# Two heads of a neighbourhood pair in one two-bank score tile, and transposes three units behind the scores

## The chip, the cores and the metric

The kernel runs on one core of one Trainium2 chip. The metric is device time in microseconds (us) of one execution. One execution computes one layer of a bidirectional encoder.

PE is the matrix engine, PEld its weight loads, DVE the vector engine, ACT the scalar engine, POOL the general engine, SP the engine whose queue issues nearly all transfers. PSUM is the memory of eight banks into which PE writes its results; DVE and ACT read them there.

## The reference, cut to what matters

The layer has two attentions over 1024 prompt tokens and 256 sample tokens, eight heads each: a neighbourhood attention (kind "n" below) and a latent attention (kind "m"). Each is scores, a softmax, and the weighted sum of values.

```python
# neighbourhood: each token looks at a window of rows and columns, with a bias
sc = jnp.einsum('bwhd,bxwyhd->bhwxy', q_r, k_nb, preferred_element_type=jnp.float32) * scale
sc = sc + bias.transpose(0, 2, 1, 3)[None].astype(jnp.float32)
p = jax.nn.softmax(sc.reshape(b, h, GRID_W, kh * NA_KW), axis=-1)
return jnp.einsum('bhwxy,bxwyhd->bwhd', p, v_nb)
...
# latent: each token looks at all tokens, in blocks of 128 queries
p = jax.nn.softmax(sc * scale, axis=-1).astype(v.dtype)
return jnp.einsum('bhqk,bkhd->bqhd', p, v)
...
# behind both: projection of each branch, a sigmoid gate from the input, merge,
# output projection, then a mixture of experts
```

## The kernel before

The program runs in stages: projections (up to 481 us of the span), attention (481 to 907), merge of the branches, routing, experts (about 1200 to 1815) and a last norm. Only the attention loop changes.

**Units.** One unit is one head (h = 2p + x, x = 0 or 1) and one block of 128 queries (qi). The two heads of a pair follow each other, so an even unit has x = 0 and an odd one x = 1. Units 0 to 63 are the latent prompt, 64 to 127 the neighbourhood prompt, 128 to 159 the sample. An "m" prompt unit has 1024 keys, in two blocks of 512, each in its own PSUM bank; an "n" prompt unit has 384 keys (256 for the first and the last block), so it fills less than one bank.

**The loop.** Iteration i does, in the order in which each engine's queue receives them: `scores` of unit i (PE) and its `maximum` (DVE; for "n" one instruction that adds the bias, writes the sum to an SBUF slot and takes the maximum, then a short read of the accumulator), `transpose` of unit i-LOOK (PE into PSUM, then a copy by ACT), `exp` of unit i (ACT), `normalize` of unit i (a reciprocal on DVE, then a multiplication on POOL), and, when unit i-LOOK-1 has x = 1, `pv` of that pair (PE). With LOOK = 2, `pv` falls into the even iterations. Then `load_at` may issue the transfers that load the next job (a head pair's q, k, v and bias), and `fill` gives PE some of 384 matmuls of the gate projection, spread over 146 iterations, so two or three an iteration (mean 2.63).

**The fill.** `piece_gates` works in pieces of 24 matmuls, so a piece lasts about nine iterations. In the middle of a piece (n == 12) the weights of the next are split into a rounded half and a remainder: a cast by ACT (L654) and a subtraction by DVE (L655), both 128x1024. These are called a burst here; in the neighbourhood prompt they come in iterations 68, 77, 86, 95, 104, 114 and 123. At a piece's end ACT copies the result out of PSUM (L682) and SP stores it to `gate_d` (L683).

**Score tiles.** `psS` has two buffers of two banks each. Every unit takes one, whatever it fills. So the scores of unit i wait until DVE has read those of unit i-2. The other four banks are taken by the transposes (2), the `pv` result (1) and the fill (1).

**Slots.** All larger SBUF data lies in 49 slots of 128x1024 that are handed out in the order in which they came free: `sl.get` and `sl.put`. A slot given back right behind the issue of a store from it is waited for by its next writer until that store has landed. The queue of SP is in order: a store to `gate_d` that stands behind a job's loads is issued behind them.

Of the kernel before, what the change touches and what calls it, by code (L numbers as in the profile page):

```python
# [10 lines left out]
F32 = mybir.dt.float32  # L11
# [84 lines left out]
def kernel(ctx, tc, A, out_p, out_s, upto=99, dbg=None):  # L96
# [14 lines left out]
    def pool(name, bufs=1, space=None, stack=None):  # L111
        kw = dict(name=name, bufs=bufs, reuse_waits="tile")
        if space is not None:
            kw["space"] = space
        return (stack or ctx).enter_context(tc.tile_pool(**kw))
# [698 lines left out]
    class Job:  # L814
# [45 lines left out]
        def vat(b, kt, h, w):  # L860
            o = kt * b.nh * 64 + (h - b.h0) * 64
            return b.v[:w, o:o + 64]

    class Unit:


# [15 lines left out]

        def scores(u):

            u.s = psS.tile([128, 2, 512], F32, name="s")
            q, k = u.job.q[u.h], u.job.k[u.h]
            qs = slice(u.qi * 128, u.qi * 128 + 128)
            for b in range(u.nb):
                ks = slice(u.t0 * 128 + b * u.w, u.t0 * 128 + (b + 1) * u.w)
                if u.kind == "m":  # L890
                    ops = [(q[0][:96, qs], k[0][:96, ks]), (q[0][:96, qs], k[1][:96, ks]), (q[1][:96, qs], k[0][:96, ks])]
                else:
                    ops = [(q[0][:, qs], k[x][:, ks]) for x in range(2)]
                for n, (a, c) in enumerate(ops):
                    PE.matmul(u.s[:, b, :u.w], a, c, start=(n == 0), stop=(n == len(ops) - 1))  # L895
# [37 lines left out]
    def pv(a, b):  # L933

        half = a.qi % 2
        key = (a.kind, a.p, a.job.g)
        if half == 0:
            oacc[key] = fps["o"][:, oturn[0] % 2, :]
            oturn[0] += 1
        o = oacc[key]  # L940
        cs = slice(half * 128, half * 128 + 128)
        for i in range(0, a.n, 128):
            w = min(128, a.n - i)
            for u in (a, b):
                PE.matmul(o[64 * u.x:64 * u.x + 64, cs], u.job.vat(u.t0 + i // 128, u.h, w), v3(u.P, 8)[:w, i // 128, :],  # L945
                          start=(i == 0), stop=(i + 128 >= a.n), tile_position=(0, 64 * u.x), skip_group_check=True)
        sl.put(a.P, b.P)
        if half:
            os = sl.get(F32R)
            t = os[:, :512].rearrange("p (x n) -> p x n", x=2)  # L950
            S.copy(t[:, 0], o)
            V.tensor_sub(t[:, 1], o, f32(t[:, 0]))
            tk = (SP if a.job.g else 0) + (a.qi - 1) * 128
            SY.dma_start(ao_d[a.kind][:, a.p * 128:a.p * 128 + 128, tk:tk + 256].rearrange("x r n -> r x n"), f32(t))
            sl.put(os)
        if b.last:
            sl.put(*b.job.t)
# [106 lines left out]
    psS = pool("psS", bufs=2, space=PSUM, stack=astack)  # L1064
# [2 lines left out]
    fps["o"] = psO.tile([128, 2, 256], F32, name="o")  # L1067
    fps["p"] = pool("psF", bufs=1, space=PSUM, stack=astack)

    LOOK = 2  # L1070
    LO, LS = (5, 5, 5, 5, 4, 4, 4), (4, 6, 4, 7)
    load_at = {16 * j + LO[j]: [jobs[j + 1]] for j in range(7)}
    load_at.update({16 * 7 + LS[0]: [jobs[8]], 16 * 7 + LS[1]: [jobs[9]], 128 + LS[2]: [jobs[10]], 128 + LS[3]: [jobs[11]]})
# [2 lines left out]
    merge = Merge()  # L1076
    for i in range(n + LOOK + 2):
        u = units[i] if i < n else None
        w = units[i - LOOK] if 0 <= i - LOOK < n else None
        z = units[i - LOOK - 1] if 0 <= i - LOOK - 1 < n else None  # L1080
        if u:
# [8 lines left out]
        if z and z.x:  # L1090
            pv(units[i - LOOK - 2], z)
        for j in load_at.get(i, []):
# [667 lines left out]
```

## Time and profile before

| | |
|---|---|
| time before, median of 3 runs | 1855.91 us (1853.6 to 1859.47) |
| the profiled execution | 1854.83 us |
| its span in the trace | 1853.1 us |
| mean granted clock of PE, as a share of full speed | 0.973 |
| PE busy | 94% of the span |
| attention in the span | 481 to 907 us |
| neighbourhood prompt units | about 723 to 853 us |

The span begins with the first instruction and ends with the last; the time of the execution is 1.7 us longer. In the rows further down a first number is the start in us from the span's start, the second the duration. A bracket tells how long the engine had been idle and which instruction ended that. "xN" is the number of instructions in a row that were put together.

### The profile page before, as it was taken

How to read it: one execution, taken by the hardware profiler on the slowest of the kernel's cores; microseconds unless marked ns; L12 is line 12 of the kernel's file. 1: busy time of each engine (PE TensorE's matmuls, PEld its weight loads, DVE VectorE, ACT ScalarE, POOL GpSimd, SP SyncE). 2: the span in 40 equal slices, each digit the busy share in tenths (PEclk: the TensorE clock that was granted, in tenths of full speed). 3: DMA queues.
4: the chain of work that ended last, by engine and by line, in shares of the span. 5: the costliest groups of instructions: out<-in, count | busy, mean ns of one | idle time of the engine just before them, and what ended most of it. 6: DMA issues, size and time to landing. Idle time of an engine off the chain costs nothing.

```text
span 1853.1 us, 27078 instructions
## 1 busy us (share of the span) xinstructions
PE 1743.1 (94%) x9874; PEld 1357.6 (73%) x9874; DVE 1001.4 (54%) x1674; ACT 838.8 (45%) x1391; POOL 319.0 (17%) x329
## 2 busy tenths in 40 slices
PE   5999999999999999999899999699999999999991
PEld 4787777998888888767688877567676676766760
DVE  6324422111455655444357466777777777777764
ACT  6222222321455555666533213366556565655642
POOL 0010210000122222322333000111111111111110
PEclk9989999999999999999899999799999999999995
DMA  9335676536714442878977356899999999999916
GB/s 349 109 115 168 222 264 221 191 91 165 152 55 112 115 121 86 232 214 230 297 251 224 132 216 235 327 359 360 361 365 360 362 356 361 358 356 364 349 36 242
DMA packets 268848, 439.47 MB, mean 237 GB/s; under 512 B 31928, under 2 KB 131592, under 8 KB 268712
## 3 DMA queue, kind: packets, MB, share of 16 engines
q1 hardware_dynamic: 252008, 389.45, 62.8%
q0 software_dynamic: 13824, 37.77, 7.3%
q10 hardware_dynamic: 2880, 10.49, 1.4%
q8 instruction: 79, 1.29, 0.3%
q14 instruction: 57, 0.47, 0.1%
HBM read 367.53 MB, written 82.67 MB: 243 GB/s over the span
## 4 chain that ended last, share of the span: by engine, by line
PE 84%; DVE 5%; DMA 5%; issue 2%; ACT 2%; SPq 1%; POOL 1%; DVEq 0%; POOLq 0%; ACTq 0%; another core or an unknown queue 0%
PE ph L1540 19%; PE pg L432 13%; PE py L1566 11%; PE s L895 6%; PE pw L1303 5%; PE fp L766 5%; PE fp L678 4%; PE o L945 4%; PE tp L927 4%; PE pg L599 3%; PE pt L1527 2%; PE pg L341 1%; PE pg L557 1%; PE pt L1553 1%; DMA x_d<-s,idx 1%
## 5 line engine op out<-in xcount | busy, mean ns | idle before, releaser
L1540 PE MATMUL ph<-s,s 128*128 128x512 f32 x1536 | 377.0, 401 | 1.4 <-DVE s L1530 1.2
L1399 ACT CAST s<-s 128x1024 fp32r<-128x1024 f32 x256 | 265.9, 1055 | 194.2 <-PE ph L1540 193.9
L1540 PEld LDWEIGHTS ph<-s,s 128*128 128x128 f32 x1536 | 286.4, 188 | 73.8 <-issue 13.9
L1400 DVE TENSOR_TENSOR s<-s,s 128x1024 fp32r<-128x1024 f32 x256 | 304.5, 1221 | 63.7 <-ACT s L1399 57.4
L432 PE MATMUL pg<-s,s 128*128 128x512 f32 (+1 forms) x1416 | 270.2, 351 | 7.8 <-ACT s L182 4.2
L432 PEld LDWEIGHTS pg<-s,s 128*128 128x128 f32 x1416 | 226.8, 190 | 53.0 <-ACT s L182 4.9
L1566 PE MATMUL py<-s,aT 128*128 128x512 f32 x512 | 225.1, 592 | 0.7 <-ACT aT L1555 0.7
L917 POOL TENSOR_SCALAR s<-s,m 128x1024 f32<-128x1024 f32 (+2 forms) x160 | 122.8, 767 | 438.5 <-DVE m L916 363.6
L1566 PEld LDWEIGHTS py<-s,aT 128*128 128x128 f32 x512 | 94.8, 190 | 108.2 <-issue 100.0
L895 PE MATMUL s<-s,s 96*128 96x512 f32 (+2 forms) x592 | 147.7, 368 | 1.8 <-ACT s L913 1.4
L913 ACT ACTIVATE s<-s,m 128x1024 f32<-128x1024 f32 (+2 forms) x160 | 124.9, 781 | 46.6 <-DVE m L903 27.3
L929 ACT COPY s<-tp 128x512 f32<-128x512 f32 (+2 forms) x160 | 78.2, 488 | 120.5 <-PE tp L927 116.9
L895 PEld LDWEIGHTS s<-s,s 96*128 96x128 f32 (+1 forms) x592 | 109.9, 190 | 27.9 <-ACT s L913 2.3
L678 PE MATMUL fp<-s,s 128*128 128x512 f32 x384 | 126.4, 430 | 2.8 <-ACT s L682 2.6
L927 PE MATMUL tp<-ident,s 128*128 128x128 f32 x752 | 110.4, 275 | 9.8 <-POOL s L917 9.4
L183 DVE TENSOR_TENSOR s<-s,s 128x1024 fp32r<-128x1024 f32 x31 | 37.7, 1224 | 148.7 <-ACT s L182 137.0
L1303 PE MATMUL pw<-s,s 128*128 128x512 f32 x480 | 118.0, 400 | 0.0
L766 PE MATMUL fp<-s,s 128*128 128x512 f32 (+1 forms) x576 | 114.0, 359 | 2.8 <-DMA s<-ao_m 1.4
L903 DVE TENSOR_REDUCE m<-s 128x1 f32<-128x1024 f32 (+1 forms) x80 | 85.0, 1062 | 51.6 <-PE s L895 50.2
L1572 POOL DMA_INDIRECT x_d<-s,idx x32 | 71.7, 2242 | 231.1 <-DVE s L1571 116.1
L766 PEld LDWEIGHTS fp<-s,s 128*128 128x128 f32 x576 | 96.5, 191 | 20.1 <-DMA s<-ao_m 2.1
L927 PEld LDWEIGHTS tp<-ident,s 128*128 128x128 f32 x752 | 89.3, 141 | 25.3 <-POOL s L917 15.9
(225 smaller groups left out, 2012.3 us busy)
## 6 DMA issues: line engine op xcount, KB each, us to landing
s<-in_expert_w SPq DMA_DIRECT2D x384, 512.0 KB
s<-in_w_in SPq DMA_DIRECT2D x47, 512.0 KB
s<-in_ada_w POOLq DMA_DIRECT2D x32, 512.0 KB, 6.1
s<-nak_d SPq DMA_DIRECT2D x40, 256.0 KB
s<-in_x_prompt SPq DMA_DIRECT2D x16, 512.0 KB
s<-in_ada_w SPq DMA_DIRECT2D x16, 512.0 KB
s<-gate_d SPq DMA_DIRECT2D x16, 512.0 KB
gate_d<-s SPq DMA_DIRECT2D x16, 384.0 KB
```

What stands on the lines that cost most here:

```text
L432: PE.matmul(p[:m, :CHUNKS[c][1]], g.at(a, j, 0, m), b.at(j, c), start=(j == 0 and n == 0), stop=(j == KD - 1 and n == 2))
L678: PE.matmul(p, w.at(a, j), b.at(j, 0), start=(n == 0), stop=(n == 23))
L766: PE.matmul(p[:, :w], b.ws[i].at(u, x * 4 + j), o[:, v, :w], start=(m == 0), stop=(m == 11))
L895: PE.matmul(u.s[:, b, :u.w], a, c, start=(n == 0), stop=(n == len(ops) - 1))
L913: S.activation(u.out, u.src, AF.Exp, bias=u.m[:, 0:1], scale=u.sign, accum_out=u.m[:, 1:2])
L917: G.tensor_scalar(u.P[:, :u.n], u.P[:, :u.n], u.m[:, 2:3], 1.0, op0=OP.mult, op1=OP.mult)
L927: PE.transpose(tp[:w, i // 128, :], u.P[:, b * 512 + i:b * 512 + i + w], ident)
L1303: PE.matmul(b.p, x[b.c].at(k, b.c, b.k), w[:, k % 2, :], start=(k + i == 0), stop=(k == 7 and i == 2))
L1399: S.copy(hi, r)
L1400: V.tensor_sub(lo, r, f32(hi))
L1540: PE.matmul(p, a[:, 2 * q + k, :], v3(w, 2)[:, k, :], start=(q + k + i == 0), stop=(q == 3 and k == 1 and i == 2))
L1566: PE.matmul(p, b.aT_[:, k, :], w[:, hb * 512:hb * 512 + 512], start=(k == 0), stop=(k == 3))
```

## The change

The two heads of a neighbourhood pair get one score tile between them: the head with x = 0 writes the first bank, the one with x = 1 the second. The latent units keep a tile each. And LOOK becomes 3, in both attentions: the transposes of a unit stand three iterations behind its scores, `pv` four, which puts `pv` into the odd iterations.

```diff
+    pairs = [None]
+
     class Unit:
...
         def scores(u):
 
-            u.s = psS.tile([128, 2, 512], F32, name="s")
+            if u.kind == "m" or u.x == 0:
+                pairs[0] = psS.tile([128, 2, 512], F32, name="s")
+            u.s = pairs[0] if u.kind == "m" else pairs[0][:, u.x:u.x + 1]
             q, k = u.job.q[u.h], u.job.k[u.h]
...
-    LOOK = 2
+    LOOK = 3
```

In the changed kernel the lines behind `scores` stand four further down (L895 becomes L899, L907 L911, L927 L931, L945 L949, L954 L958); L654, L655, L678, L682 and L683 keep their numbers. In the rows below a name with a number is one buffer or tile, the text in brackets what the instruction waits for, by the engine or transfer queue that has to finish.

The first place is PE's queue, units 92 and 93, the end of a `pv` and the second head's scores, before:

```order
L945 MATMUL o_3905<-s48_6960,s7_6518 64x128
L945 MATMUL o_3905<-s23_6983,s7_6518 64x128
L678 MATMUL fp_7061<-s47_399,s37_6936 128x512 [waits Activation_49]
L678 MATMUL fp_7061<-s31_413,s37_6936 128x512
L678 MATMUL fp_7061<-s47_399,s15_6937 128x512
L678 MATMUL fp_7061<-s47_399,s37_6936 128x512
L895 MATMUL s_7068<-s33_6512,s8_6509 128x384 [waits DVE_49]
L895 MATMUL s_7068<-s16_6515,s8_6509 128x384
L927 MATMUL tp_7074<-ident_63,s41_7026 128x128 [waits PE_49,Pool_49]
L927 MATMUL tp_7074<-ident_63,s41_7026 128x128 x2
```

The same two units in the changed kernel, from the first head's scores to those of the second and the start of the `pv` behind them:

```order
L899 MATMUL s_7022<-s28_6492,s3_6489 128x384
L899 MATMUL s_7022<-s15_6495,s3_6489 128x384
L931 MATMUL tp_7028<-ident_63,s37_6959 128x128 [waits PE_49,Pool_49]
L931 MATMUL tp_7028<-ident_63,s37_6959 128x128 x2
L678 MATMUL fp_7036<-s47_399,s42_6910 128x512 [waits Activation_49]
L678 MATMUL fp_7036<-s31_413,s42_6910 128x512
L678 MATMUL fp_7036<-s47_399,s1_6911 128x512
L678 MATMUL fp_7036<-s47_399,s42_6910 128x512
L899 MATMUL s_7022<-s8_6501,s13_6498 128x384 [waits DVE_49]
L899 MATMUL s_7022<-s25_6504,s13_6498 128x384
L931 MATMUL tp_7048<-ident_63,s44_6981 128x128 [waits PE_49,Pool_49]
L931 MATMUL tp_7048<-ident_63,s44_6981 128x128 x2
```

Both heads write the tile s_7022. The first waits for no engine; the second waits for DVE, whose last instruction on that tile is the first head's maximum (L911) just ahead. Before, the wait of the second head (tile s_7068) was for the unit two earlier. And `pv` stands behind the second head's scores now, where it stood behind the first one's.

The second place is DVE's queue at units 108 and 109, before (slot and score tile are the first names behind the operation and the arrow):

```order
L907 ISA s13_7409,m_7410<-s_7406,s20_6886 128x384 [waits PE_49,Pool_49]
L907 ISA m_7410 128x1
L916 RECIPROCAL m_7410<-m_7410 128x1 [waits Activation_49]
L907 ISA s26_7431,m_7432<-s_7428,s42_6888 128x384 [waits PE_49,Pool_49]
L907 ISA m_7432 128x1
```

And in the changed kernel, from the end of unit 107 to unit 108:

```order
L920 RECIPROCAL m_7356<-m_7356 128x1 [waits Activation_49]
L956 TENSOR_TENSOR s11_7372<-o_3905,s11_7372 128x256 [waits Activation_49]
L911 ISA s46_7382,m_7383<-s_7379,s4_6867 128x384 [waits DMAHW7_49,PE_49,Pool_49]
L911 ISA m_7383 128x1
L920 RECIPROCAL m_7383<-m_7383 128x1 [waits Activation_49]
```

The maximum of unit 108 now writes slot s46 and waits for a transfer from it. That transfer stands in SP's queue, in the changed kernel, behind the loads of the next job:

```order
L807 DMA s16_7215<-nak_d 64x1024 [waits DMAHW3_49]
L844 DMA s18_7218<-vna_d 128x8x128 [waits DMAHW4_49]
L857 DMA s48_7220<-in_nbias 128x768 [waits DMAHW5_49]
L857 DMA s33_7222<-in_nbias 128x768 [waits DMAHW6_49,PE_49,Pool_49]
L683 DMA gate_d<-s46_7225 128x512 [waits DMAHW7_49,Activation_49]
L650 DMA s6_7250<-in_w_in 128x8x128 [waits DMAHW0_49,PE_49,Pool_49]
```

Before, the store at this place was from slot s24, and the next to write s24 was the copy L682 of the piece that ends in iteration 109, on ACT, with the same wait. In the same way the maximum of unit 124 waits in the changed kernel for the store of the piece that ends in iteration 118, and the subtraction L655 of iteration 95 for an `ao_n` store.

## Rows read from the trace of the kernel before

**Rows 1.** The page: busy us of each engine, share of the span, instructions.

```profile
PE 1743.1 (94%) x9874; PEld 1357.6 (73%) x9874; DVE 1001.4 (54%) x1674; ACT 838.8 (45%) x1391; POOL 319.0 (17%) x329
```

**Rows 2.** Busy time by stretch: columns in the first line; stretches of attention.

```profile
core 0: us, PE busy (x) PEld busy (x) DVE busy (x) ACT busy (x) POOL busy (x), PEclk, DMA share, GB/s
...
500.00:723.00 223.00, 223.00 (x1871) 189.66 (x1870) 127.01 (x192) 116.23 (x200) 64.27 (x58) 1.00 0.39 102
...
800.00:820.00 20.00, 18.12 (x138) 14.20 (x136) 8.50 (x32) 12.56 (x34) 5.51 (x10) 1.00 1.04 275
...
894.00:900.00 6.00, 5.09 (x24) 3.87 (x24) 2.25 (x10) 2.76 (x10) 5.60 (x11) 0.50 0.95 326
```

**Rows 3.** Waits, 723 to 853: us in total, times, longest us.

```profile
PE tp L927 <- POOL s L917: 4.9, 6, 1.2
...
PE fp L678 <- ACT s L682: 2.6, 3, 1.8
...
ACT s L682 <- DMA gate_d<-s: 2.1, 1, 2.1
```

**Rows 4.** Waits, 853 to 907, columns as in the group above.

```profile
PE tp L927 <- POOL s L917: 4.4, 8, 1.1
...
PE s L895 <- ACT s L913: 1.4, 1, 1.4
```

**Rows 5.** Timeline, a pair without a burst: start us, us, engine, line, operation.

```profile
749.97 0.51 PE L895 MATMUL s<-s,s 128*128 128x384 f32 x2
...
750.63 0.56 DVE L907 CUSTOM_DVE_ANT_0 s<-s,s 128x384 f32<-128x384 f32 x1 [0.24 <-POOL s L917]
...
751.11 0.08 DVE L907 DVE_READ_ACCUMULATOR2_ANT m<- 128x1 f32 x1
751.11 0.51 PE L895 MATMUL s<-s,s 128*128 128x384 f32 x2
...
753.49 0.52 PE L895 MATMUL s<-s,s 128*128 128x384 f32 x2
...
754.87 0.40 PE L895 MATMUL s<-s,s 128*128 128x256 f32 x2
```

**Rows 6.** Timeline, the burst of iteration 68.

```profile
735.87 0.52 PE L895 MATMUL s<-s,s 128*128 128x384 f32 x2
...
738.03 0.51 PE L895 MATMUL s<-s,s 128*128 128x384 f32 x2
738.09 1.03 ACT L654 CAST s<-s 128x1024 fp32r<-128x1024 f32 x1
...
740.77 0.08 DVE L907 DVE_READ_ACCUMULATOR2_ANT m<- 128x1 f32 x1
...
742.23 0.08 DVE L907 DVE_READ_ACCUMULATOR2_ANT m<- 128x1 f32 x1
```

**Rows 7.** Timeline, scores that waited for a maximum, after the burst of iteration 95.

```profile
792.15 0.08 DVE L907 DVE_READ_ACCUMULATOR2_ANT m<- 128x1 f32 x1
...
792.28 0.61 PE L895 MATMUL s<-s,s 128*128 128x384 f32 x2 [0.37 <-DVE m L907]
```

**Rows 8.** Timeline, 795 to 819: scores of unit 99, SP's stores, unit 108's maximum, L682.

```profile
795.54 0.52 PE L895 MATMUL s<-s,s 128*128 128x384 f32 x2
...
796.32 0.36 SPq L954 DMA_DIRECT2D ao_n<-s  x1
...
808.33 0.33 SPq L683 DMA_DIRECT2D gate_d<-s  x1
...
813.13 0.56 DVE L907 CUSTOM_DVE_ANT_0 s<-s,s 128x384 f32<-128x384 f32 x1
...
818.02 0.58 ACT L682 COPY s<-fp 128x512 f32<-128x512 f32 x1 [2.09 <-DMA gate_d<-s]
```

**Rows 9.** Timeline, 843 to 846: the store of iteration 118, unit 124's maximum.

```profile
843.85 0.33 SPq L683 DMA_DIRECT2D gate_d<-s  x1
...
845.69 0.55 DVE L907 CUSTOM_DVE_ANT_0 s<-s,s 128x384 f32<-128x384 f32 x1
```

## The prediction

> **What bounds the kernel now.** I read the page first: PE is busy for 94% of the span [rows 1], so the change can only win idle time of PE, and loses where it makes more. Next the busy times by stretch. In the latent prompt units PE is busy for 223.00 of 223.00 us [rows 2]: nothing is to be won there, and a unit's PE work is long enough to hide any of its waits. In the neighbourhood prompt units PE has gaps; the waits name them [rows 3]: six waits of the transposes for POOL's multiplication, 4.9 us, and three of the fill for ACT's copy L682, 2.6, of which one, 1.8, is ACT's own 2.1 us wait for a `gate_d` store. One wait of scores for a maximum adds 0.37 [rows 7]. That makes 7.9 us. In the sample units it is 4.4 for POOL and 1.4 for an exponential [rows 4]. So all that the change could win is 7.9 + 5.8 = 13.7 us, 0.74%.
>
> Then the timeline, to see how far PE may run ahead of DVE. In a pair without a burst the scores of one unit start at 749.97, its maximum at 750.63, the read of the accumulator ends at 751.11 + 0.08 = 751.19, and PE starts the next unit's scores at 751.11, with two fill matmuls between [rows 5]. With three it takes 754.87 - 753.49 = 1.38 [rows 5]; with `pv` 753.49 - 751.11 = 2.38 [rows 5] or 738.03 - 735.87 = 2.16 [rows 6]. Mean of an iteration without `pv` (1.14 and 1.38, at 2.63 fills a mean) 1.29, with `pv` 2.27.
>
> **What the change adds: a wait for the unit just ahead.** In the changed order the second head's scores wait for DVE, and the last that DVE does on the shared tile is the first head's maximum. Before, scores waited for the maximum of two units earlier. So at each odd unit PE leads DVE by one unit, not two; and since `pv` moves to the odd iterations, what lies between the two heads' scores is the short iteration.
>
> *Ordinary pairs.* The wait lets go at 751.19 plus what rows 7 show between the end of a read (792.15 + 0.08 = 792.23) and the scores it releases (792.28), 0.05: 1.27 behind the first head's scores. That is 0.13 more than the iteration with two fills and less than that with three. Of 32 pairs some 37% have two, less those in bursts 9: 9 x 0.13 = 1.2 us.
>
> *Bursts.* In iteration 68 the scores start at 735.87, the cast L654 at A = 738.09, 2.2 later; in other bursts I take 2.0 to 2.2. DVE then does L655 before the next two maxima, whose reads end at 740.77 + 0.08 = 740.85 (A + 2.76) and 742.23 + 0.08 = 742.31 (A + 4.22) [rows 6]. Before, PE had two units of lead and lost only the 0.6 us or so that the late multiplication cost. With the shared tile:
> - burst in an odd iteration b (77, 95, 123): the scores of b+2 wait for the maximum of b+1, until A + 2.81, or 4.8 to 5.0 behind the scores of b. PE wants them after an iteration with `pv` and one without, 2.27 + 1.29 = 3.56. Stall 1.25 to 1.45, taken 1.35.
> - burst in an even iteration (68, 86, 104, 114): the scores of b+3 wait for the maximum of b+2, until A + 4.27, or 6.3 to 6.5; wanted after 1.29 + 2.27 + 1.29 = 4.85. Stall 1.4 to 1.6, taken 1.5.
>
> Together 3 x 1.35 + 4 x 1.5 = 10.0 us, from 8.5 (the least of each, and some slack) to 12.
>
> **What it takes away.** With transposes three behind, POOL has a whole iteration more; I count the 4.9 us and the 0.37 as gone: -5.3. The two small waits for L682 (2.6 - 1.8 = 0.8) lose perhaps 0.3, as ACT has more slack.
>
> **What it moves: slots.** One more unit's slot is alive, so slots return later, and the order in which they return shifts. Three writers that did not wait for a store now have a store ahead of them; each is followed by scores that wait for it.
> - Unit 108's maximum waits for the `gate_d` store behind the job loads of iteration 100. Before, that store was issued at 808.33 and let go ACT's L682 at 818.02 [rows 8], 21.7 behind the `ao_n` store at 796.32 that precedes the loads. That `ao_n` store now comes from an odd iteration, 99, some 2.9 behind its scores (two fills, transposes, `pv`, ACT and DVE), so the store lands some 24.6 behind the scores of unit 99. Unit 108's maximum was 813.13 - 795.54 = 17.6 behind them [rows 8]; with the stall of the burst of 104 and two of 0.1 it is 19.3. It waits 5.3 us, and PE with it, through the scores of 109; what L682 waited there before (1.8) goes. Net +3.4; ends 0 (landed in time, less the 1.8: -1.8) and +6.
> - Unit 124's maximum waits for the store issued at 843.85, when that maximum stood at 845.69 [rows 9]. No row shows when this one landed; with 9.7 from issue to release in the row above as the upper end and nothing as the lower, I take 5.5. The loads ahead of it come an iteration later, +1, so it lands near 850.4, and the maximum would stand near 847 with the stalls so far. +3, from 0 to +6.
> - L655 of iteration 95: 0.3.
>
> **Sample units.** Both waits are there too, the lead is the same; POOL has its other work there. -1 to -3 from later transposes, and up to +2 from a store that an exponential of unit 144 may wait for; I take 0.
>
> **The sum.** -5.3 - 0.3 + 10.0 + 1.2 + 3.4 + 3.0 + 0.3 = +12.3 us. Behind attention no instruction changes, and its stages wait for attention's results, so I carry the loss to the end. Against the profiled execution, 1854.83 + 12.3 = 1867.1; the median shown is 1.1 above that execution, and I state 1867.
>
> **A page against the rows.** Scores were held until 0.05 us behind a maximum [rows 7]; that was a reuse of the same tile, and no row of before shows two heads in one. The Trainium skill, "PSUM — Partial Sum Buffer", section "Summary: rules for kernel authors", says that PSUM which is being read while a matmul runs should be left alone by aiming the matmul at a different bank, and that semaphores guard by bank. By that the second head, which writes the other bank, need not wait: the wait is then the program's, not the chip's, and without it the sum would be that of rival A. The changed order has the wait, so the sum goes by the held scores.
>
> **Rivals.**
> - *A. It does what four scores in PSUM promise: faster.* If the second head's wait is met before PE gets there also in bursts (it decides at the burst: the maximum of b+1 done by 3.6 behind the scores of b, where rows 6 give 4.8), the 5.3 goes and of the sample's 5.8 some 2: 1854.83 - 7.3 = 1847.5, and at best 1841.1. Against it: L655 alone keeps DVE for 1.23 us more than a maximum. The Trainium skill, "Perfetto Trace Analysis", section "Optimization Strategy", has a rule for it: a gap that repeats on the engine that should be saturated can mean too little PSUM for the next tile. Here the gaps name POOL and not a tile, but for one of 0.37 us [rows 3, 7].
> - *B. Waits trade places.* Stalls in bursts come out at half (5) because ACT's copies move off the chain, and the stores land in time: -5.6 + 5 + 1.2 - 1.8 = -1, about 1854 to 1858.
> - *C. Only the shared tile's wait costs.* Stores land in time, bursts as above: -5.6 + 11.2 = +5.6, with L682's wait kept or gone 1858.6 to 1860.4.
> - *D. As forecast, and the clock falls.* In the sample's end PE's gaps were followed by a stretch, 894 to 900, with a granted clock of 0.50 (1.2 GHz), in which 5.1 us of PE work were done at that level [rows 2]. A stall of 5 us at unit 108 could bring the like; half of such a stretch is lost, 2.6 us or more, at one or two places: 1870 to 1875.
>
> **How the numbers follow.** Forecast as summed (with one of the two stores late or both) 0.47, C 0.18, D 0.10, B 0.14, A 0.11. Of C some 0.10 lies within 0.3% (5.6 us), about what a measurement of this kernel can tell from no change. So faster 0.11, same 0.24, slower 0.65. The forecast's own range is 1861 to 1874; the stated one, 1855 to 1876, leaves out A, the best of B and the worst of D.
>
> **What would show it.** In the profile of after: scores L899 waiting for DVE L911 in 723 to 853, some 10 us or more in at least seven places of over 1 us behind L654 and L655; L921's waits before the transposes L931 near zero; L911 of unit 108 waiting for a `gate_d` store for some 5 us, and of unit 124 for some 3; the latent prompt still without a gap. It is wrong if the scores' waits sum to less than 6 us, or if the transposes still wait for POOL, or if stores let go in time.

## The result

The changed kernel took 1877.22 us (median of 4 runs, 1876.42 to 1878.24) against 1855.32 for the kernel before (4 runs): a ratio of 1.0115, 95% interval 1.0097 to 1.0133. It is slower by 21.9 us. I had stated 1867, from 1855 to 1876: the direction is right, the size is not, and the time lies 1.2 us above the range.

The profiled execution took 1878.24 us, its span is 1876.5. The page, first line of busy times, has PE busy for 8.6 us more than in [rows 1], with the same 9874 matmuls:

```profile
PE 1751.7 (93%) x9874; PEld 1362.9 (73%) x9874; DVE 1002.0 (53%) x1674; ACT 839.4 (45%) x1391; POOL 319.7 (17%) x329
```

So the loss is not idle time alone. I cut the span at the first scores and at the end of the last `pv`. Busy times by stretch, changed kernel (the columns of [rows 2]):

```profile
484.54:927.96 443.42, 415.20 (x3235) 339.10 (x3233) 224.60 (x519) 248.05 (x554) 131.32 (x174) 0.98 0.57 150
...
815.00:820.00 5.00, 3.85 (x28) 2.81 (x27) 1.96 (x8) 3.26 (x10) 1.76 (x3) 1.00 1.09 244
820.00:825.30 5.30, 0.00 (x0) 0.00 (x0) 0.57 (x2) 0.09 (x1) 0.00 (x0) 0.78 1.08 363
825.30:828.00 2.70, 2.67 (x15) 2.24 (x17) 0.73 (x3) 1.63 (x5) 0.58 (x1) 0.50 0.20 70
...
830.00:832.00 2.00, 2.00 (x15) 1.47 (x15) 0.94 (x4) 1.29 (x5) 0.00 (x0) 1.00 0.36 135
```

And the same cut in the kernel before:

```profile
480.99:905.61 424.62, 410.01 (x3235) 336.65 (x3233) 223.66 (x519) 247.39 (x554) 130.33 (x174) 0.99 0.59 157
```

Attention is 443.42 - 424.62 = 18.8 us longer. In it PE is busy for 415.20 us instead of 410.01, with the same number of matmuls: 5.2 us more, which further down the granted clock accounts for; its gaps grew from 14.6 to 28.2 us, by 13.6. The 4.6 us that are left lie in the stages ahead of attention (it begins 3.5 us later) and behind it (1.1 longer), whose instructions did not change.

The waits of the changed kernel from 723 to 880 us, the neighbourhood prompt units, answer to [rows 3]:

```profile
PE s L899 <- DVE m L911: 18.7, 9, 5.9
...
DVE s L911 <- DMA gate_d<-s: 10.0, 2, 5.6
...
PE s L899 <- DMA ao_n<-s: 1.0, 1, 1.0
```

Neither the transposes' wait for POOL nor the fill's for L682 is in the list any more. In their place PE's scores wait for a maximum, nine times. PE's timeline has the places:

```profile
746.11 0.62 PE L899 MATMUL s<-s,s 128*128 128x384 f32 x2 [1.29 <-DVE m L911]
...
816.20 0.61 PE L899 MATMUL s<-s,s 128*128 128x384 f32 x2 [1.13 <-DVE m L911]
...
825.33 1.01 PE L899 MATMUL s<-s,s 128*128 128x384 f32 x2 [5.34 <-DVE m L911]
843.22 0.85 PE L899 MATMUL s<-s,s 128*128 128x384 f32 x2 [1.99 <-DVE m L911]
...
865.24 1.01 PE L899 MATMUL s<-s,s 128*128 128x384 f32 x2 [5.87 <-DVE m L911]
```

The row at 816.20 is the burst of iteration 104: L655 keeps DVE from 812.98, the maximum of the next unit starts at 814.12, that of the one behind it at 815.58, and only then may the second head's scores start. The row at 825.33 is unit 109. Its pair's first head, unit 108, has its maximum held by a store. DVE's timeline there:

```profile
818.64 0.42 DVE L956 TENSOR_TENSOR s<-o,s 128x256 fp32r<-128x256 f32 x1
824.71 0.56 DVE L911 CUSTOM_DVE_ANT_0 s<-s,s 128x384 f32<-128x384 f32 x1 [5.64 <-DMA gate_d<-s]
825.19 0.08 DVE L911 DVE_READ_ACCUMULATOR2_ANT m<- 128x1 f32 x1
```

And the chain that ended last in the stretch 815 to 830 (start us, us, what) begins with that store, 9.61 us from its issue:

```profile
814.93 9.61 DMA gate_d<-s
824.55 0.03 issue
```

Read the rows of the stretches again with this: nothing at all ran on PE from 820.00 to 825.30, the DMA share was 1.08, and in the 2.7 us behind it the granted clock was 0.50, the lower of the two levels (1.2 GHz). The scores there took 1.01 us for two, where they take 0.62 after a shorter wait. In attention the changed kernel has four stretches at 0.50 (columns as above):

```profile
822.95:829.78 6.83, 4.45 (x21) 3.50 (x22) 1.46 (x6) 1.92 (x6) 1.17 (x2) 0.50 0.47 147
843.43:846.84 3.41, 3.41 (x16) 2.46 (x16) 0.89 (x4) 1.56 (x5) 1.15 (x2) 0.50 0.81 207
863.91:870.74 6.83, 5.50 (x26) 4.46 (x26) 1.69 (x7) 1.79 (x5) 1.17 (x2) 0.50 0.39 121
918.52:921.94 3.42, 3.42 (x20) 2.76 (x20) 1.61 (x7) 2.15 (x8) 3.31 (x5) 0.50 1.05 398
```

The kernel before has one there:

```profile
893.28:900.10 6.82, 5.49 (x25) 4.27 (x26) 2.57 (x11) 3.49 (x13) 5.66 (x11) 0.50 0.95 331
```

PE worked 16.8 us at the lower level in the changed kernel and 5.5 before. Half of the difference, 5.6 us, is an estimate of what the clock cost more; PE's busy time grew by 5.2.

### The profile page after: what moved, and what is told of

It is laid out like the page before. It is cut to its first block, busy times and chain, and to the rows that moved or that the text cites. A ratio compares the mean times of both kernels' runs of the same rounds, so it can differ in the third digit from the quotient of the medians.

```text
span 1876.5 us, 27068 instructions
## 1 busy us (share of the span) xinstructions
PE 1751.7 (93%) x9874; PEld 1362.9 (73%) x9874; DVE 1002.0 (53%) x1674; ACT 839.4 (45%) x1391; POOL 319.7 (17%) x329
## 3 DMA queue, kind: packets, MB, share of 16 engines
q8 instruction: 79, 1.29, 0.3%
## 4 chain that ended last, share of the span: by engine, by line
PE 84%; DMA 5%; DVE 5%; issue 2%; ACT 2%; SPq 1%; POOL 0%; DVEq 0%; POOLq 0%; ACTq 0%; another core or an unknown queue 0%
PE ph L1544 18%; PE pg L432 13%; PE py L1570 11%; PE s L899 6%; PE pw L1307 5%; PE fp L766 5%; PE o L949 5%; PE fp L678 4%; PE tp L931 4%; PE pg L599 3%; PE pt L1531 2%; PE pg L341 1%; DMA gate_d<-s 1%; PE pg L557 1%; PE pt L1557 1%
## 5 line engine op out<-in xcount | busy, mean ns | idle before, releaser
L899 PE MATMUL s<-s,s 96*128 96x512 f32 (+2 forms) x592 | 150.6, 373 | 27.5 <-DVE m L911 25.7
L899 PEld LDWEIGHTS s<-s,s 96*128 96x128 f32 (+1 forms) x592 | 108.5, 191 | 60.8 <-DVE m L911 36.2
L678 PE MATMUL fp<-s,s 128*128 128x512 f32 x384 | 128.1, 434 | 0.1
L907 DVE TENSOR_REDUCE m<-s 128x1 f32<-128x1024 f32 (+1 forms) x80 | 85.0, 1062 | 49.7 <-PE s L899 48.3
L931 PE MATMUL tp<-ident,s 128*128 128x128 f32 x752 | 110.0, 275 | 0.0
L1307 PEld LDWEIGHTS pw<-s,s 128*128 128x128 f32 x480 | 89.8, 191 | 19.5 <-issue 1.4
```

The lines of the kernel that those rows point to most:

```text
L678: PE.matmul(p, w.at(a, j), b.at(j, 0), start=(n == 0), stop=(n == 23))
L931: PE.transpose(tp[:w, i // 128, :], u.P[:, b * 512 + i:b * 512 + i + w], ident)
L1307: PE.matmul(b.p, x[b.c].at(k, b.c, b.k), w[:, k % 2, :], start=(k + i == 0), stop=(k == 7 and i == 2))
```

## The experiments

Each run was timed beside the kernel before on its chip. "Attention" below is the cut shown above, with PE's busy time and the rest as gaps, from one profiled execution each; the last column is the ratio of all runs, with its interval. The median of the kernel before was 1855.3 beside the changed kernel, 1855.9 beside runs 1 to 4, 1854.5 beside 5 to 8 and 1855.2 beside 9 to 12.

| kernel | median us | attention | PE busy | gaps | ratio to before |
|---|---|---|---|---|---|
| before (LOOK 2, own tiles) | 1855.3 | 424.6 | 410.0 | 14.6 | |
| changed (LOOK 3, shared) | 1877.2 | 443.4 | 415.2 | 28.2 | 1.0115 [1.0097, 1.0133] |
| 1: LOOK 3, own tiles | 1869.2 | 437.8 | 413.4 | 24.4 | 1.0067 [1.0041, 1.0092] |
| 2: LOOK 2, shared | 1855.4 | 423.9 | 409.4 | 14.5 | 0.9996 [0.9985, 1.0008] |
| 3: changed, gate slot held | 1859.7 | 432.6 | 413.0 | 19.6 | 1.0019 [1.0006, 1.0032] |
| 4: LOOK 3, four tiles, gate slot held | 1857.6 | 428.0 | 412.0 | 16.0 | 1.0013 [1.0000, 1.0027] |
| 5: changed again | 1873.3 | 444.6 | 415.5 | 29.1 | 1.0096 [1.0078, 1.0114] |
| 6: changed, bursts in quarters | 1874.5 | 442.9 | 415.7 | 27.2 | 1.0112 [1.0083, 1.0142] |
| 7: before, quarters, gate slot held | 1854.4 | 422.9 | 411.1 | 11.8 | 0.9993 [0.9982, 1.0003] |
| 8: as 4, quarters | 1858.7 | 427.5 | 410.6 | 16.9 | 1.0022 [1.0009, 1.0036] |
| 9: changed, both slots held | 1858.9 | 429.2 | 411.5 | 17.7 | 1.0021 [1.0009, 1.0032] |
| 10: LOOK 3, own tiles, both held | 1849.1 | 418.1 | 407.0 | 11.1 | 0.9964 [0.9948, 0.9980] |
| 11: as 7, both held | 1848.5 | 420.3 | 410.3 | 10.0 | 0.9966 [0.9955, 0.9978] |
| 12: as 8, both held | 1847.0 | 416.6 | 407.0 | 9.6 | 0.9965 [0.9946, 0.9983] |

**The first four: one part at a time.** Run 1 undoes the sharing, run 2 the look-ahead:

```diff
-            if u.kind == "m" or u.x == 0:
-                pairs[0] = psS.tile([128, 2, 512], F32, name="s")
-            u.s = pairs[0] if u.kind == "m" else pairs[0][:, u.x:u.x + 1]
+            u.s = psS.tile([128, 2, 512], F32, name="s")
```

```diff
-    LOOK = 3
+    LOOK = 2
```

Run 3 keeps the change and gives a `gate_d` store's slot back one piece later, so that its next writer comes long after the store has landed:

```diff
-                        sl.put(t)
+                        if held[0] is not None:
+                            sl.put(held[0])
+                        held[0] = t
```

Run 4 has that too, and from unit 64 on a pool of four tiles of one bank, one for each unit, in place of the two of two banks:

```diff
+        if i == 64:
+            sstack.close()
+            psS[:] = [pool("psN", bufs=4, space=PSUM, stack=sstack), 1]
...
+            u.s = psS[0].tile([128, psS[1], 512], F32, name="s")
```

> LOOK = 3 alone, a tile for each unit as before. Theory (the loss is three things: the second head's wait for the first head's maximum, two waits for gate_d stores, and a clock that falls behind such stalls): the transposes' waits for POOL go (4.9 and 4.4 us), the scores' waits at the seven bursts shrink from about 1.2 us each to a sum under 2 us, the waits of the maxima of units 108 and 124 for their stores stay and cost PE one iteration less each (3 to 4 us instead of 5.3 and 5.9), with less or no fall of the clock: 1852 to 1862 us. Rival (the longer look-ahead itself costs the time, the tile is innocent): 1872 us or more, with the same gaps as the changed kernel.

> The shared tile alone, LOOK = 2. Theory: pv stays in the even iterations, so the long iteration lies between the two heads' scores and the wait for the first head's maximum costs nothing in ordinary pairs; at a burst 0.5 us (even iteration) or 1.3 us (odd), partly in the place of the transposes' waits; slots as before, so one stall of 1.8 us and no more; clock as before: 1855 to 1861 us. Rival (the tile costs its full 10 us wherever pv stands): 1864 us or more.

> The changed kernel, but the slot of a gate_d store is given back one piece (nine iterations) later, so that nobody waits for that store. Theory: the maxima of units 108 and 124 wait for no transfer; PE's stalls of 5.3 and 5.9 us shrink to the burst's share (0 and 1.3), and the stretches at half clock behind them go: 15 us less than the changed kernel, 1859 to 1866 us. Rival (the stalls would come anyway, from the bursts and the shared tile): 1872 us or more.

> LOOK = 3, from unit 64 on four score tiles of one bank each (no tile is shared), and the slot of a gate_d store given back one piece later. Theory: neither the second head's wait nor the stores' waits are left, and the transposes do not wait for POOL: of the 13.7 us of gaps that the kernel before has in the neighbourhood and sample units 8 to 12 go: 1842 to 1849 us. Rival (the longer look-ahead costs by itself, through slots or the order of the queues): 1855 us or more.

Run 2 came as expected: with LOOK = 2, where `pv` lies between the two heads' scores, the shared tile costs nothing in sum. It is not free of waits. From 723 to 853 the scores wait for a maximum seven times, and the transposes, which wait 4.9 us for POOL in [rows 3], no longer do; the two waits trade places:

```profile
PE s L899 <- DVE m L911: 5.5, 7, 1.2
PE fp L678 <- ACT s L682: 2.2, 3, 1.4
```

Run 3 came as expected too: a ratio of 1.0019 instead of 1.0115, from the one kind of slot. In attention it wins back 10.8 of the 18.8 us, so more than half of the loss is stores, with the clock behind their stalls. Run 1 missed: 1869.2 where 1852 to 1862 was expected, near the rival's 1872. Its waits from 723 to 880 say why:

```profile
DVE s L909 <- DMA gate_d<-s: 14.3, 2, 8.1
PE s L897 <- DVE m L909: 12.4, 3, 7.2
```

The stores are waited for longer than in the changed kernel (14.3 us against 10.0): with own tiles PE loses less at the bursts and comes to the same stores earlier, and its stalls there, 4.96 and 7.24 us, are in sum 1 us longer than the 5.34 and 5.87 of the changed kernel. I had reckoned with one iteration less of stall at each; that was wrong. Run 4 missed as well, 1857.6 where 1842 to 1849 was expected: with the `gate_d` slots out of the way, ACT waited for `ao_n` stores instead, 2.13 us ahead of L654 at 795.85 and 2.52 ahead of a cast at 857.62.

**The next four.** Run 5 is the changed kernel unchanged, for a second profile. In runs 6 to 8 the burst's two instructions are cut into four pieces of 128x256, which stand at n = 8, 11, 14 and 17 of a fill piece:

```diff
+        def part(b, k):
+            if k == 0:
+                b.p = [sl.get(F32R), sl.get(F32R)]
+            c = slice(k * 256, k * 256 + 256)
+            S.copy(b.p[0][:, c], b.raw[:, c])
+            V.tensor_sub(b.p[1][:, c], b.raw[:, c], f32(b.p[0])[:, c])
...
-                    if n == 12 and k + 1 < 16:
-                        ps[k + 1].split()
+                    if n in (8, 11, 14, 17) and k + 1 < 16:
+                        ps[k + 1].part((8, 11, 14, 17).index(n))
```

> The changed kernel once more, for a second profile. Of the 23.4 us by which its first profiled span was longer, 18.8 lay in attention (14.0 of gaps, 4.8 of PE work at a lower clock) and 4.6 in the stages ahead of and behind it, which have the same instructions. Theory: the 18.8 are the change's and come again within 1 us; the 4.6 are not, and come out anywhere from -3 to +6. Rival (the change also slows the stages around it): 4 to 6 us outside attention again, and a start of attention at 484 us or later.

> The changed kernel, with each burst (L654 and L655, 128x1024) cut into four parts of 128x256 that stand in four iterations. Theory: the waits of the scores at the seven bursts, 9 us in sum, fall below 3, because no maximum stands behind a 1.2 us subtraction any more; the two stalls for gate_d stores stay (about 5 us each) with the half clock behind them: 1865 to 1871 us. Rival (the shared tile binds in every pair, bursts or not): 1874 us or more.

> The kernel before, bursts in quarters and the slot of a gate_d store given back one piece later. Theory: the gaps of the kernel before in the neighbourhood prompt (7.9 us) have the same two sources as the changed kernel's, the bursts and the gate_d slot; both go, 5 to 8 us less in attention: 1847 to 1852 us. Rival (the gaps are the depth of the look-ahead and stay): 1854 us or more.

> LOOK = 3, four score tiles of one bank, slot held (as the fourth run), and the bursts in quarters. Theory: in that run PE, freed of the tile, ran ahead until the fill's one bank and pv's bank held it at the bursts (about 12 us of gaps in the neighbourhood prompt); with the bursts spread these go: 1846 to 1852 us. Rival (LOOK = 3 costs by itself): 1856 us or more.

Run 5: attention 444.6 us again, 20.0 longer than before (1.2 more than the first time), while it began at 481.35, not at 484.5, and the stages behind it were 1.3 us shorter than in the kernel before. So the 4.6 us outside attention are not shown to be the change's.

Run 6 missed, and is the one from which I learned most. The bursts' waits fell as expected, to between 0.17 and 0.38 us in the rows of its timeline up to 778 us, and yet the time is that of run 5. PE's timeline:

```profile
794.84 0.51 PE L908 MATMUL s<-s,s 128*128 128x256 f32 x2 [2.43 <-DVE m L920]
...
823.60 1.01 PE L908 MATMUL s<-s,s 128*128 128x384 f32 x2 [6.33 <-DVE m L920]
...
861.91 1.01 PE L908 MATMUL s<-s,s 128*128 128x384 f32 x2 [6.42 <-DVE m L920]
```

The stalls behind the stores are 6.33 and 6.42 us, where the two profiles of the changed kernel have 5.34 and 5.87, and 5.26 and 6.95; one of 2.43, in place of 1.04, has an `ao_n` store ahead of it. What PE saved ahead of the first store it waited for there: the scores of unit 109 start 340.6 us behind the first scores of attention in run 6, 340.7 in run 5. Behind the second store run 6 is 3.1 us ahead of run 5, and 1.4 of that are lost again by the end of attention.

Runs 7 and 8 missed too: 1854.4 for 1847 to 1852, 1858.7 for 1846 to 1852. In run 7, from 723 to 856, no `gate_d` store is waited for, but the transposes still wait for POOL, 3.6 us against 4.9 before; spread bursts do not take that wait away with LOOK = 2:

```profile
PE tp L940 <- POOL s L930: 3.6, 9, 0.8
PE fp L688 <- ACT s L692: 1.3, 3, 0.6
```

In run 8 the holder is in DVE's and PE's timeline, a part of the burst that writes a slot from which an `ao_n` store had not landed, and behind it the subtraction L967, for which `pv` waits:

```profile
794.06 0.43 DVE L663 TENSOR_TENSOR s<-s,s 128x256 fp32r<-128x256 f32 x1 [3.61 <-DMA ao_n<-s]
795.75 0.43 DVE L967 TENSOR_TENSOR s<-o,s 128x256 fp32r<-128x256 f32 x1
...
796.23 1.13 PE L960 MATMUL o<-s,s 128*64 128x128 f32 x7 [2.60 <-DVE s L967]
```

**The last four: hardly a store is waited for.** They hold the slots of `ao` stores too, until two more such stores have been issued:

```diff
-            sl.put(os)
+            heldo.append(os)
+            if len(heldo) > 2:
+                sl.put(heldo.pop(0))
```

> The changed kernel, with the slots of gate_d stores given back one piece later and those of ao stores two stores later. Theory: no instruction of the attention loop waits for a store; what is left are the second head's waits at the seven bursts (9 us) and in the sample units: attention about 429 us long (before 424.6, changed 443.4 and 444.6), 1855 to 1860 us. Rival (a third of the loss is neither tile nor slot): 1864 us or more.

> LOOK = 3 alone with own tiles, and both kinds of slots held. Theory: LOOK = 3 with own tiles lost 13 us by waits for stores alone (5.0 and 7.2 us of gaps and the half clock behind them); without them the transposes' waits are gone and little has come for them: attention 420 to 426 us, 1850 to 1857 us. Rival (the look-ahead has another cost): 1862 us or more.

> The kernel before, bursts in quarters, both kinds of slots held. In its seventh run sister (only gate_d held) attention was 422.9 us long against 424.6. Theory: the last wait for an ao store goes too (1.35 us of ACT), some 1 us: 1851 to 1855 us, faster than before by 0 to 0.2%. Rival (slots held longer make the loads wait instead): 1857 us or more.

> LOOK = 3, four tiles of one bank, bursts in quarters, both kinds of slots held. In the eighth run (only gate_d held) two waits for ao stores were left, 3.6 us of DVE and 2.5 of ACT, with PE gaps of 2.6 and 2.8 us and a half clock behind each. Theory: these go with what followed, 8 to 10 us less in attention than that run's 427.5: 418 to 421 us, 1847 to 1852 us, the best of all. Rival (PE then waits elsewhere, at the fill's one bank): attention 424 us or more, 1854 us or more.

Now the runs come near the theory: 1858.9 and 1847.0 are as expected, 1849.1 and 1848.5 are 0.9 and 2.5 us under the stretch given. Attention of run 9 is 429.2 as expected, of run 10 418.1 and of run 12 416.6, 2 and 1.4 us below what I gave. For run 11 I had reckoned with 1 us less than run 7; it took 5.9 less, of which 2.6 lie in attention, and what the rest is stays open. Run 9 against run 10 is the shared tile alone, with LOOK = 3: 9.8 us of time; in attention 11.1, 6.6 of gaps and 4.5 of PE's busy time. Waits of run 9, from 723 to 880:

```profile
PE s L903 <- DVE m L915: 11.0, 10, 2.0
...
DVE s L915 <- DMA ao_n<-s: 0.7, 1, 0.7
```

And of run 10, same stretch:

```profile
PE fp L679 <- ACT s L683: 4.3, 7, 1.0
PE o L952 <- DVE s L959: 1.5, 3, 0.5
...
PE s L901 <- DVE m L913: 0.2, 1, 0.2
```

With own tiles the scores hardly wait; PE is held by the fill's one bank (its copy is ACT's) or by `pv`'s bank instead. So part of what the shared tile costs is owed elsewhere anyway.

In run 12 each unit has a bank of its own. DVE reads one while PE writes the next, in the timeline at 755 us, where the two overlap:

```profile
755.76 0.42 DVE L922 CUSTOM_DVE_ANT_0 s<-s,s 128x256 f32<-128x256 f32 x1
755.89 0.40 PE L910 MATMUL s<-s,s 128*128 128x256 f32 x2
```

Runs 10, 11 and 12 beat the kernel before by 0.34 to 0.36%; their intervals overlap, so which of them is best stays open. Run 11 has neither LOOK = 3 nor other tiles.

## Why the prediction was off

- **The second head's wait.** Right in mechanism and near in size: 11.2 us forecast (10.0 at bursts, 1.2 in ordinary pairs). Run 9 has 11.0 us of such waits, 9.4 at the seven bursts, 0.6 in ordinary pairs and 1.0 in the sample units, which the 11.2 left out. That runs 9 and 10 differ by 9.8 us of time is in part luck: of the 11.1 in attention only 6.6 are gaps. In the changed kernel the bursts of 68 to 104 stalled PE for 1.29, 1.11, 1.35, 1.04 and 1.13 us; that of 114 for 1.99. The ordinary pairs cost 0.6 us there too (two waits of 0.31 in 32 pairs), half of the 1.2.
- **The transposes' waits.** Right: none is left in the prompt. Their worth, with L682's stall, was -7.4 us in the forecast. Run 10 is 6.1 us faster than the kernel before beside it, but that the two are near is luck: its attention has only 3.5 us less of gaps, since PE waits elsewhere, and 3.0 less of PE's busy time.
- **Unit 108's store.** Right: 5.3 us forecast, 5.34 and 5.26 measured in the two profiles. The store let go 9.61 us behind its issue, as in [rows 8] (9.69).
- **Unit 124's store.** Too small: 3 us beyond the burst. Measured 5.87 and 6.95, with the burst 1.37 (run 9, same place): 4.5 and 5.6. The store, issued at 858.90, let the maximum start at 864.62, 5.7 later, where I had taken 5.5; but that maximum was due 1.3 us behind the issue, not 2.2.
- **Sample units.** I took 0. The gaps of PE there sum to 7.8 us in the rows of the timeline, against 6.1 before. The longest is the second head's wait behind a burst and not for a store: run 9 has it too, with the same 3.33 us. In the changed kernel:

```profile
914.26 1.40 DVE L655 TENSOR_TENSOR s<-s,s 128x1024 fp32r<-128x1024 f32 x1 [0.77 <-ACT s L654]
917.71 0.50 PE L899 MATMUL s<-s,s 128*128 128x256 f32 x2 [3.33 <-DVE m L911]
```

- **All gaps together.** 12.3 us forecast, 13.6 measured in the first profile. Terms that came out too large (bursts, ordinary pairs, L655 of iteration 95) and too small (unit 124, the sample) cancel in part, so the sum is closer than its terms. With 13.6 in it the time would have been about 1868.
- **The step that failed: the clock.** The sum had no term for it; it put the clock at nothing and left it to rival D, 2.6 us at one or two places, with a chance of 0.10. The runs showed 5.2 us more of PE's busy time in the first profile and 5.5 in the second, at the same number of matmuls. D's price for a place was right: half of the work done at 0.50 in the four stretches is 2.2, 1.7, 2.8 and 1.7 us, an estimate. The number of places was wrong: four, where the kernel before has one (2.7 us), behind the stalls of 5.34, 1.99 and 5.87 us and of 3.33 at 917.71. I thought of a stall of 5 us; one of 1.99 was followed by it as well. With the measured 5.2 or 5.5 in the sum the forecast would have been 1872 or 1873, near the 1873.3 of run 5 and 4 to 5 us below the first result.
- **What stays open.** In the first measurement the medians differ by 21.9 us and the two profiles' attention by 18.8; in the second it is 18.8 between medians of 1873.3 and 1854.5, and 20.0 in attention. The median of the same changed kernel moved by 3.9 us between the two. What lies outside attention has the same instructions, and no run shows why it was longer the first time.

The clock came mostly with the stores. Their part was forecast as 8.5 us (5.2, 3.0 and 0.3); from the changed kernel to run 9 the time falls by 18.3 us from the first median and 14.4 from the second. In attention it is 14.2: 10.5 us of gaps and 3.7 of PE's busy time. Of the four stretches at 0.50 run 9 has two left, behind the stalls of 1.99 and 3.33 us; the two behind the stores' stalls are gone. Of the rivals, A (no wait at all) is refuted by the rows at the bursts, C (the tile's wait alone) is what run 9 is, at 1858.9 where C had 1858.6 to 1860.4, though 1.5 of its 4.6 us in attention are PE's busy time and not gaps, and D is what happened, at more places than D had.

On the rule of the Trainium skill in "PSUM — Partial Sum Buffer", section "Summary: rules for kernel authors" (aim the matmul at a different bank than the one being read): the trace of run 12 agrees, with a 0.40 us score into one bank that starts 0.13 us into a 0.42 us read of another. The wait in the changed kernel came from the tile that both banks belong to. The Trainium skill, "Perfetto Trace Analysis", section "Optimization Strategy", says that repeating gaps can mean too little SBUF or PSUM for the next tile. Where the scores waited for a tile the traces agree: with a tile for each unit the gaps of run 9 fall from 17.7 to 11.1 us in run 10. For the other gaps no run shows it: run 12, with four score tiles, and run 11, with two, have 9.6 and 10.0 us, and they differ in LOOK too.

## What to carry to other kernels

When a buffer goes back to a free list right behind the issue of a store from it, its next writer waits until the store has landed, so a change that keeps one more buffer alive can put that wait on the path of the bound engine; holding such slots a little longer took 14 to 20 us off the kernels with LOOK = 3. Two halves of one tile were one thing to the waits, so give each writer a tile of its own, or put the long work between the two. And gaps ahead of a fixed landing do not add up: what is saved in front of it is waited for at it.

## What the runs showed of the hardware

A stall can cost twice. In the neighbourhood prompt of these runs PE's gaps of 1.04 to 1.41 us, and one of 1.83 in the kernel before (816.83), were not followed by a fall of the granted clock to 0.50; with those of 1.99 us and more, but for one (2.43 us in run 6), it fell for 3.4 to 10.2 us. The length of one gap does not settle it: in the sample units the clock fell with one of 1.41 us (kernel before, 892.29), and in run 4 behind two of 0.84 and 0.76. Attention in the second profile of the changed kernel, by stretch:

```profile
481.35:925.96 444.61, 415.53 (x3235) 340.23 (x3233) 224.45 (x519) 248.03 (x554) 131.28 (x174) 0.97 0.56 150
```

Run 10, with no gap above 1.03 us in the prompt, does the same 3235 matmuls in 407.00 us of PE time: 3 us less than the kernel before and 8.5 less than this row. Its clock falls once, as in the kernel before, but PE does 3.4 us of work in that stretch and not 5.5; by half of the difference that is 1 us of the 3, an estimate, and the rest is not worked out.
